# Encoder trunk on one core: dilated V, partial sums and K swaps in fewer transfers, and new priorities and a margin in the order planner

## The chip, the cores and the metric

The kernel runs on one core of a Trainium2 chip. The metric is the device time of one execution in microseconds (us). Engines are named as in the profile: PE is TensorE (PEld its weight loads), DVE is VectorE, ACT is ScalarE, POOL is GpSimd, SP is SyncE, which here issues every DMA (SPq in the rows). All DMAs of the core share 16 DMA engines.

## The reference, cut to what matters

Two request groups, a prompt of 512 rows and a sample of 1024 rows, go through the same two layers with a model width of 1024.

- Layer 0: `h = rms_norm(x)`, `z = h @ w_in0`, split into A (8 query heads over 2 key/value heads, norm on q and k, two-dimensional rotary), B (4 heads of differential attention, two softmaxes subtracted) and a gate; `x + ((A || B) * silu(gate)) @ w_out0`.
- Layer 1: `z = h @ w_in1` gives q, k, v and gate for 16 heads. Attention C has three patterns, (window, dilation) = (128, 1), (512, 4), (2048, 16), each a band in a strided copy of the sequence, merged by their softmax denominators: `o = sum(softmax(lse)[i] * o_i)`. Then `x + (o * silu(gate)) @ w_out1`.

All inputs are fp32. The kernel keeps precision by splitting every fp32 operand into two fp16 parts (high and low) and making three passes of each product (`mm3`, `av`).

## The kernel before, in words

**Units and pieces.** Layer 0 has four A units and four B units, layer 1 has eight C units (two heads each). A unit is made of three pieces of 512 rows (`GRAN`): piece 0 is the prompt, pieces 1 and 2 are the two halves of the sample. `kv_piece` projects K and V of a piece, `qg_piece` q and the gate; `qk_stages` squares, makes 1/rms on POOL (`f_chain`), applies the rotary, splits into fp16 parts and transposes by DMA into `K` or `q` (line 594). The projections of the next unit are merged with the attention steps of this one, so that PE has dense work (line 492) between the short products of the attention.

**Attention step.** Scores on PE into `S` (2 buffers), maximum on DVE, exponential on ACT into `f`, high part on ACT and low part on DVE or POOL into `h` (3 buffers), then a DMA transpose `t<-h` (line 359, called from `t_av`) into `t` (3 buffers, token `t4`), then the product with V on PE (line 784, `av`). `out_tile` has the same transpose for the output projection.

**What C adds.** For the dilated patterns V is needed by class (row modulo 4). Line 682 copies each 128-row tile of `V` into 32 partitions of `Vc`: four transfers for a piece, 96 in all. The dilated partial output lies by class too; `send` (line 1152) puts it back in row order, `pk` to `pn`, in four transfers of 32 partitions, 96 in all. For the scores the two heads' halves of K are also needed swapped: lines 599 and 600 copy partitions 64 to 127 of each new K piece to 0 to 63 of the other slot and the reverse, 78 in all.

**What sets the order.** Nothing is scheduled on the chip. At build time `Plan.run` plays the stages through a model of the engines, with estimated durations and latencies, and writes the instructions in the order in which the model starts them. Each engine, SP too, then runs its own list in that order and only waits for semaphores. Among the stages that are ready, each engine of the model takes the one with the lowest `pos`; `P.pos` grows by 1 with each merged step. A stage that acquires a token starts only when a buffer of that kind is free in the model (`CAPS`). `P.dma` makes three stages: SP issue, DMA, and a latency stage that occupies nothing ("LAT"); the DMA stage can start 0.75 us after the issue (`LAT0`), and the latency is 1.25 us unless a line says otherwise; `P.tdma` is the same for a transpose, with lengths by columns.

**The end of a layer** is written out by hand in `END`: the last units' attention with what projections remain, the weights of the output projection (`wprep`, line 423 its sum of squares, lines 432 to 435 the sum over partitions on PE) and the output tiles.

Of the kernel before, what the change touches and what calls it, by code (L numbers as in the profile page):

```python
# [183 lines left out]


ISSUE = 0.6
PA, PQ, PB = 0, 8, 0
KEEP1 = 1

# [24 lines left out]
def trunk_kernel(ctx: ExitStack, tc: tile.TileContext, A: dict, outs: list):  # L214
    nc = tc.nc
# [298 lines left out]
        return r  # L514


    def qk_stages(zb, ztok, evs, e2, tabs, tdep, ti, kind, isq, dst, dst_acq, dst_use, swap, dst_dep=()):

        b = {}
        t1t, stt_ = Token("t1"), Token("st")  # L520

        def f_sq():
            b["t1"] = new(t1t)
            S_.activation(out=b["t1"], in_=zb["z"], func=AF.Square)
        s = add("ACT", act(512), f_sq, evs, [t1t], [ztok])

        def f_red():
            b["s"] = small(24, "qs", 6)
            V.tensor_reduce(out=b["s"][:, 0:8], in_=b["t1"].rearrange("p h t d -> p (h t) d"), op=AD, axis=AX.X)  # L529
        s = add("DVE", dve(512), f_red, [s], (), [t1t])  # L530

        def f_chain():

            x = b["s"]
            G.tensor_scalar(out=x[:, 8:16], in0=x[:, 0:8], scalar1=1.0 / (64.0 * 4096.0 ** 2), scalar2=e2(), op0=M, op1=AD)  # L535
            rsqrt(x[:, 0:8], x[:, 16:24], x[:, 8:16], 8)
        sr = add("POOL", 3.6, f_chain, [s])

        def t1f():
            return b["t1"].rearrange("p h t d -> p (h t) d")  # L540

        if kind == "A":
            s1t = Token("s1")

            def f_rope():
                gc_t, gs_t = tabs()
                z, t1 = zb["z"], b["t1"]
                s1 = lpool[0].tile([128, 2, 4, 64], F32, tag=f"s1{s1t.slot}", name="s1", bufs=1)
                tt(t1, z, gc_t[:, ti:ti + 4, :].unsqueeze(1).to_broadcast([128, 2, 4, 64]), M)
                zs = z.rearrange("p h t (s y d) -> p (h t s) y d", s=2, y=2)[:, :, ::-1, :]  # L550
                s1v = s1.rearrange("p h t (s y d) -> p (h t s) y d", s=2, y=2)
                for h in range(2):
                    gsv = gs_t[:, ti:ti + 4, :].rearrange("p t (s y d) -> p (t s) y d", s=2, y=2)
                    tt(s1v[:, 8 * h:8 * h + 8], zs[:, 8 * h:8 * h + 8], gsv, M)
                tt(t1, t1, s1, AD)
            sp = add("DVE", 2 * dve(512) + 2 * dve(256) + 0.1, f_rope, [s, tdep], [s1t], [t1t, ztok])

            def f_r():
                tt(t1f(), t1f(), b["s"][:, 0:8].unsqueeze(2).to_broadcast([128, 8, 64]), M)
            s = add("DVE", dve(512), f_r, [sp, sr], (), [t1t])  # L560
        else:
            s1t = Token("s1")

            def f_rope():
                gc_t, gs_t = tabs()[0:2]
                z, t1 = zb["z"], b["t1"]
                tt(t1f(), z.rearrange("p h t d -> p (h t) d"),
                   b["s"][:, 0:8].unsqueeze(2).to_broadcast([128, 8, 64]), M)
                s1 = lpool[0].tile([128, 2, 4, 16], F32, tag=f"s1{s1t.slot}", name="s1", bufs=1)
                ts_ = t1.rearrange("p h t d -> p (h t) d")[:, :, 0:16].rearrange("p a (y d) -> p a y d", y=2)[:, :, ::-1, :]  # L570
                s1v = s1.rearrange("p h t (y d) -> p (h t) y d", y=2)
                for h in range(2):
                    tt(s1v[:, 4 * h:4 * h + 4], ts_[:, 4 * h:4 * h + 4],
                       gs_t[:, ti:ti + 4, :].rearrange("p t (y d) -> p t y d", y=2), M)
                tt(t1[:, :, :, 0:16], t1[:, :, :, 0:16],
                   gc_t[:, ti:ti + 4, :].unsqueeze(1).to_broadcast([128, 2, 4, 16]), M)
                if isq:
                    tt(t1f()[:, :, 16:64], t1f()[:, :, 16:64],
                       tabs()[2][:, 16:64].unsqueeze(1).to_broadcast([128, 8, 48]), M)
                tt(t1[:, :, :, 0:16], t1[:, :, :, 0:16], s1, AD)  # L580
            s = add("DVE", dve(512) + 2 * dve(64) + 2 * dve(128) + 0.3 + (dve(384) if isq else 0.0), f_rope, [sr, tdep], [s1t],
                    [t1t, ztok])

        def f_hi():
            b["st"] = new(stt_)
            S_.activation(out=b["st"][:, :, :, 0:64], in_=b["t1"], func=AF.Copy)
        s = add("ACT", act(512), f_hi, [s], [stt_], [t1t])

        def f_lo():
            tt(b["st"][:, :, :, 64:128], b["t1"], b["st"][:, :, :, 0:64], SU)  # L590
        s = add("DVE", dve(512), f_lo, [s], (), [t1t, stt_])

        def f_T():
            nc.sync.dma_start_transpose(out=dst().rearrange("p h (t q) -> p (h t) q", q=128),
                                        in_=b["st"].rearrange("p h t c -> p (h t c)"))
        s = P.tdma(1024, f_T, [s, dst_dep], dst_acq, tuple(x for x in dst_use if x not in dst_acq) + (stt_,))
        if swap is None:
            return [s]
        w1 = dma(ISSUE, 0.25, lambda: nc.sync.dma_start(out=swap()[0:64], in_=dst()[64:128]), [s], (), dst_use)
        w2 = dma(ISSUE, 0.25, lambda: nc.sync.dma_start(out=swap()[64:128], in_=dst()[0:64]), [s], (), dst_use)  # L600
        return [s, w1, w2]


    class Unit:
        def __init__(self):
# [1 line left out]
            self.qtok, self.sgtok = {}, {}  # L607
            self.k_ready, self.v_ready, self.vc_ready = {}, {}, {}
            self.att_done = {}
            self.Vc = [None, None]  # L610

    last_mm = [None]
    proj_mm = {}
# [10 lines left out]
    def kv_piece(u, gi):  # L624
# [4 lines left out]
        for hf in range(2):  # L629
# [41 lines left out]
                    in1=u.V[:, r:r + 2, 0, :], op0=M, op1=SU)  # L671
            vl = add("DVE", dve(256), f_vl, [vh], (), [pt, u.vtok], pos=P.pos - PB)
            vls.append(vl)
            if u.kind == "C":
                for j in range(2):
                    tl = t0 + 2 * hf + j

                    def f_vc(tl=tl, r=r, j=j):
                        if u.Vc[g] is None:
                            u.Vc[g] = lpool[0].tile([128, g + 1, 4, 256], F16, tag=f"Vc{g + 1}{u.vct[g].slot}", name=f"Vc{g + 1}", bufs=1)  # L680
                        p0 = 32 * (tl % 4)
                        nc.sync.dma_start(out=u.Vc[g][p0:p0 + 32, tl // 4, :, :],
                                          in_=u.V[:, r + j, :, :].rearrange("p a f -> p (a f)"))
                    if tl == 0:
                        u.vc_open = add("NONE", 0.0, None, [vl, u.tdep], [u.vct[g]])
                    vc = dma(ISSUE, 0.25, f_vc, [vl, u.vc_open], (), [u.vct[g], u.vtok])
                    u.vc_ready.setdefault(g, []).append(vc)
        u.v_ready[gi] = vls
        def kdst():
            if not hasattr(u, "K"):  # L690
                u.K = new(u.ktok)
            return u.K[:, 0, gi]
        u.k_ready[gi] = qk_stages(zb, ztok, evs, lambda: u.kvw.e2, lambda: u.ktab, u.tdep, t0, u.kind, False,
                                  kdst, [u.ktok] if gi == 0 else (), [u.ktok], lambda: u.K[:, 1, gi],
                                  () if gi == 0 else u.k_ready[0][0])
        if gi == 2:
            w_done(u.kvw, mms)
# [1 line left out]
    def qg_piece(u, gi):  # L699
# [57 lines left out]
        def qdst():  # L757
            if gi not in u.q:
# [1 line left out]
            return u.q[gi]  # L760
        ti = row // 128 if u.kind == "C" else t0
        u.q_ready[gi] = qk_stages(zb, ztok, evs, lambda: u.qgw.e2, lambda: u.qtab, u.tdep, ti, u.kind, True,
                                  qdst, (), [qt], None)
        if gi == 2:
            w_done(u.qgw, mms)

# [37 lines left out]
    def t_av(u, b, s, h4t, av_fn, av_dur, av_deps, av_acq=(), av_use=()):  # L804
        t4t = Token("t4")

        def f_T():
            b["tt"] = transp(b["hl"], t4t)
        s = P.tdma(2048, f_T, [s], [t4t], [h4t])
        return add("PE", av_dur, av_fn, [s, av_deps], av_acq, [t4t] + list(av_use))  # L810

    def spill(l, u, gi, dep):
# [253 lines left out]
    def att_C(u, gi):  # L1066
# [46 lines left out]
        def p23(hs):  # L1113
            def build():
# [15 lines left out]
                def avf(t4):  # L1130
                    if "o23" not in ob:
                        ob["o23"] = new(ot23).rearrange("p a b -> p (a b)").rearrange("p (c h d) -> p c h d", c=4, h=2)
                    for i, (h, c) in enumerate(blocks):
                        av(ob["o23"][:, c, h, :], t4, i * L // 128, L // 128,
                           lambda k, b: u.Vc[g][:, k, c, 128 * b + 64 * h:128 * b + 64 * h + 64])
                batch(mm, len(blocks) * pe(2 * L, 2), blocks, L, lambda x: u.m23[g][:, t0 // 4, :], mxs,
                      lambda x: ob["md"][:, x[1], 2 + x[0]:3 + x[0]], avf, [u.vc_ready[g]], avs23, ot23)
            return build
# [1 line left out]
        def send():  # L1140
# [2 lines left out]
                S_.activation(out=ob["pk"][:, :, 128:132], in_=ob["md"], func=AF.Copy)  # L1143
                S_.activation(out=ob["pk"][:, :, 0:128], in_=ob["o23"].rearrange("p c h d -> p c (h d)"), func=AF.Copy)
            s = add("ACT", act(512) + 0.12, f_ev, avs23[-1:], [pkt], [ot23])
            s = add("NONE", 0.0, None, [s], [pnt])
            ob["sent"] = []
            for j in range(4):
                def f(j=j):
                    if j == 0:  # L1150
                        ob["pn"] = lpool[0].tile([128, 4, 132], F32, tag=f"pn{pnt.slot}", name="pn", bufs=1)
                    nc.sync.dma_start(out=ob["pn"][:, j, :],
                                      in_=ob["pk"][32 * j:32 * j + 32, :, :].rearrange("p c f -> p (c f)"))
                ob["sent"].append(dma(ISSUE, 0.25, f, [s], (), [pkt, pnt]))
            if gi == 0 or gi == 2:
                close(u.vct[g], avs23)

# [103 lines left out]
    def out_tile(l, g, tl, wo, mix_deps, x_deps, finish):  # L1261
# [31 lines left out]

        def f_T():
            b["tt"] = transp(b["hl"], t4t)
        s = P.tdma(2048, f_T, [s], [t4t], [h4t])

        def f_x():
            x = b["x"] = new(xt)
# [417 lines left out]
```

## Time and profile before

| what | value |
|---|---|
| median of 3 runs | 1854.68 us (1853.79 to 1855.3) |
| profiled execution, its time | 1854.62 us |
| profiled execution, its span | 1852.4 us |
| PE busy | 1675.0 us, 90% |
| DVE / ACT / POOL busy | 1332.2 / 1212.8 / 695.5 us |
| mean granted clock of PE | 0.959 of full speed |

The span runs from the first to the last instruction; the time includes 2.2 us around it. Matmuls are pipelined and their ends are modelled, so the busy time of PE says how much of the span has a matmul in it. An idle time of an engine is put down to what ended it, the releaser.

### The profile page before, as it was taken

The numbers are of one execution on the slowest core, as the hardware profiler recorded it, in microseconds if no ns is written. First come the engines' busy times: TensorE is split into PE (matmuls) and PEld (weight loads), VectorE is DVE, ScalarE is ACT, GpSimd is POOL, SyncE is SP. The second block draws the span as 40 slices with busy tenths as digits, with TensorE's granted clock in tenths as the row PEclk, the third lists the DMA queues.
The fourth block names the chain that finished last, engine by engine and source line by source line (L and its number), as shares of the span: only waits on it lengthen the run. The fifth ranks groups of instructions, "written<-read, shape, count | busy, mean of one in ns | idle before, by whom it ended". The sixth has DMA issues, their size and how long they took to land. (4 is left out here: it accounts for less than half of the span.)

```text
span 1852.4 us, 44798 instructions
## 1 busy us (share of the span) xinstructions
PE 1675.0 (90%) x17626; PEld 1398.4 (75%) x17626; DVE 1332.2 (72%) x2985; ACT 1212.8 (65%) x2593; POOL 695.5 (38%) x1204
## 2 busy tenths in 40 slices
PE   4898978989999999699898999999999999995898
PEld 3776756878887878378787887888788888774788
DVE  7788878767888778965635778677777777787332
ACT  6488978767777767853425676678676757777220
POOL 6523333333463445312212344354444444452200
PEclk9999999999999999799899999999999999996999
DMA  9989999795565445689975676676766757776983
GB/s 251 191 157 166 182 177 167 146 163 113 98 125 101 109 92 122 147 198 224 207 176 128 122 150 131 138 143 140 147 132 144 137 116 151 148 145 140 232 230 103
DMA packets 788724, 282.06 MB, mean 152 GB/s; under 512 B 647072, under 2 KB 772256, under 8 KB 788512
## 3 DMA queue, kind: packets, MB, share of 16 engines
q1 hardware_dynamic: 788512, 279.19, 73.4%
q8 instruction: 138, 2.26, 0.5%
q14 instruction: 74, 0.61, 0.1%
HBM read 73.92 MB, written 25.17 MB: 53 GB/s over the span
## 5 line engine op out<-in xcount | busy, mean ns | idle before, releaser
L492 PE MATMUL pj<-whl,hT 128*128 128x256 f16 x7680 | 882.3, 275 | 22.2 <-DMA hT<-h 21.2
L492 PEld LDWEIGHTS <-hT 128*128 128x128 f16 x7968 | 782.8, 99 | 145.6 <-DMA hT<-h 23.1
L784 PEld LDWEIGHTS <-t 128*128 128x128 f16 x4992 | 200.5, 100 | 93.8 <-DMA t<-h 85.8
L1107 ACT ACTIVATE f<-f,cs,csc 128x256 f32<-128x256 f32 (+1 forms) x384 | 218.4, 570 | 65.5 <-DVE cs L778 65.4
L492 PEld LDWEIGHTS <-t 128*128 128x128 f16 x2304 | 228.9, 100 | 40.0 <-DMA t<-h 9.8
L800 DVE TENSOR_TENSOR h<-f,h 128x1024 f16<-128x1024 f32 x148 | 187.7, 1273 | 57.4 <-ACT h L796 55.0
L784 PE MATMUL pj<-V,t 128*128 128x64 f16 (+1 forms) x4032 | 178.7, 204 | 51.2 <-DMA t<-h 47.8
L492 PE MATMUL pj<-whl,t 128*128 128x256 f16 x1728 | 202.4, 279 | 8.2 <-DMA t<-h 8.2
L772 PE MATMUL S<-K,q 128*128 128x512 f16 x640 | 169.6, 399 | 33.3 <-ACT f L1024 19.1
L796 ACT ACTIVATE h<-f 128x1024 f16<-128x1024 f32 x168 | 175.5, 1051 | 21.9 <-DMA t<-h 19.8
L535 POOL TENSOR_SCALAR qs<-qs,we 128x8 f32<-128x8 f32 x87 | 44.5, 511 | 354.0 <-DVE qs L529 343.1
L261 POOL TENSOR_TENSOR qs<-qs,mhalf 128x8 f32<-128x8 f32 x87 | 147.8, 1699 | 7.3
L772 PEld LDWEIGHTS <-q 128*128 128x128 f16 x640 | 61.0, 101 | 91.7 <-issue 42.8
L854 DVE TENSOR_REDUCE as<-S 128x1 f32<-128x1024 f32 (+1 forms) x80 | 95.9, 1219 | 29.1 <-PE S L772 28.9
L423 ACT ACTIVATE t<-f 128x1024 bf16<-128x1024 f32 x74 | 77.8, 1051 | 44.5 <-DMA f<-in_w_in_dram 32.6
L864 ACT ACTIVATE f<-S,as,asc 128x1024 f32<-128x1024 f32 (+1 forms) x96 | 101.7, 1061 | 4.0 <-DVE h L800 0.5
L478 DVE SCALAR_TENSOR_TENSOR whl<-f,wsm,whl 128x1024 f16<-128x1024 f32 x68 | 87.7, 1305 | 8.2 <-ACT whl L473 8.2
L1332 DVE SCALAR_TENSOR_TENSOR f<-pj,os,f 128x256 f32<-128x256 f32 x96 | 41.9, 479 | 68.0 <-PE pj L492 61.2
L1018 DVE TENSOR_REDUCE bs<-S 128x1 f32<-128x1024 f32 x64 | 77.2, 1217 | 16.2 <-PE S L772 16.2
L800 POOL TENSOR_TENSOR h<-f,h 128x1024 f16<-128x1024 f32 x20 | 43.5, 2175 | 120.9 <-ACT h L796 120.9
L473 ACT ACTIVATE whl<-f,wsm 128x1024 f16<-128x1024 f32 x68 | 75.8, 1140 | 16.8 <-PE pj L492 14.3
L1122 PE MATMUL S<-K,q 128*128 128x256 f16 (+1 forms) x384 | 79.3, 371 | 4.6 <-DVE m L1097 4.6
(250 smaller groups left out, 2684.5 us busy)
## 6 DMA issues: line engine op xcount, KB each, us to landing
f<-in_w_in_dram SPq DMA_DIRECT2D x58, 512.0 KB, 5.3
mixbuf<-sg SPq DMA_DIRECT2D x48, 256.0 KB, 2.8
f<-mixbuf SPq DMA_DIRECT2D x24, 512.0 KB, 5.7
K<-K SPq DMA_DIRECT2D x78, 128.0 KB, 2.5
f<-in_w_out_dram SPq DMA_DIRECT2D x16, 512.0 KB, 4.5
pn<-pk SPq DMA_DIRECT2D x96, 66.0 KB, 2.2
x1buf<-f SPq DMA_DIRECT2D x12, 512.0 KB, 4.1
Vc<-V SPq DMA_DIRECT2D x96, 64.0 KB, 2.3
```

What stands on the lines that cost most here:

```text
L261: G.tensor_tensor(y, v, mhalf[:, 0:n], ALU.pow)
L423: S_.activation(out=junk1(t1t), in_=b[i].rearrange("p k n -> p (k n)"), func=AF.Square, accum_out=b["s"][:, i:i + 1])
L478: stt(out=part(k, 1, i), in0=b[i][:, nk * k:nk * k + nk, :], scalar=sc(), in1=part(k, 0, i), op0=M, op1=SU)
L492: T.matmul(ps, lhs(k, a), wt(k, b), start=(k == 0 and i == 0), stop=(k == 7 and i == 2))
L772: T.matmul(out[:, 512 * i:512 * i + 512], q, u.K[:, st, gi, hk, :], start=(st == 0), stop=(st == 1))
L784: T.matmul(o, t4[:, 8 * a + base + k, :], v(k, b), start=(k == 0 and i == 0), stop=(k == nk - 1 and i == 2))
L796: S_.activation(out=b["hl"][:, 0, :], in_=b["e"], func=AF.Copy)
L800: (G if on_pool else V).tensor_tensor(b["hl"][:, 1, :], b["e"], b["hl"][:, 0, :], SU)
L854: V.tensor_reduce(out=b["s"][:, 0:nh], in_=b["S"].rearrange("p (h k) -> p h k", h=nh), op=ALU.max, axis=AX.X)
L864: S_.activation(out=b["e"][:, w * i:w * i + w], in_=b["S"][:, w * i:w * i + w], func=AF.Exp, bias=b["s"][:, 2 + i:3 + i], scale=u.sc, accu ...
L1107: S_.activation(out=b["e"][:, w * i:w * i + w], in_=b["e"][:, w * i:w * i + w], func=AF.Exp, bias=b["s"][:, i:i + 1], scale=u.sc, accum_ou ...
L1122: T.matmul(s[:, L * i:L * i + L], q, k, start=(sk == 0), stop=(sk == 1))
```

## The change

In the model (`Plan`), which only sets the order:

- the 1/rms chains of `qk_stages` (POOL) get a `pos` lower by 12;
- the transposes of K and q, of the attention tiles (`t_av`) and of the output tiles (`out_tile`) get a `pos` lower by 10;
- behind each transpose of an attention or output tile stands a latency stage of `AHEAD = 2.5` us, in which the `t4` buffer stays taken; the product that reads the tile may start in the model only after it.

In the transfers:

- V by class: one store of the whole piece to a DRAM buffer `vd` (256 KB) and one load back with four rows to a partition, instead of four copies of 64 KB. `Vc` is one tile per piece instead of one per group.
- partial sums: one store of `pk` to a DRAM buffer `pd` and one load into `pn`, instead of four copies; `pn` is now acquired by the load alone.
- K swaps: none after piece 1; after piece 2 both sample pieces are swapped with one pair of transfers of double size.

```diff
+AHEAD = 2.5
@@ qk_stages
-        sr = add("POOL", 3.6, f_chain, [s])
+        sr = add("POOL", 3.6, f_chain, [s], pos=P.pos - 12)
...
-        s = P.tdma(1024, f_T, [s, dst_dep], dst_acq, tuple(x for x in dst_use if x not in dst_acq) + (stt_,))
+        s = P.tdma(1024, f_T, [s, dst_dep], dst_acq, tuple(x for x in dst_use if x not in dst_acq) + (stt_,), pos=P.pos - 10)
         if swap is None:
             return [s]
-        w1 = dma(ISSUE, 0.25, lambda: nc.sync.dma_start(out=swap()[0:64], in_=dst()[64:128]), [s], (), dst_use)
-        w2 = dma(ISSUE, 0.25, lambda: nc.sync.dma_start(out=swap()[64:128], in_=dst()[0:64]), [s], (), dst_use)
-        return [s, w1, w2]
+        return [s] + swap(s)
@@ kv_piece
-            if u.kind == "C":
-                for j in range(2):
-                    tl = t0 + 2 * hf + j
-
-                    def f_vc(tl=tl, r=r, j=j):
...
-                        p0 = 32 * (tl % 4)
-                        nc.sync.dma_start(out=u.Vc[g][p0:p0 + 32, tl // 4, :, :],
-                                          in_=u.V[:, r + j, :, :].rearrange("p a f -> p (a f)"))
-                    if tl == 0:
-                        u.vc_open = add("NONE", 0.0, None, [vl, u.tdep], [u.vct[g]])
-                    vc = dma(ISSUE, 0.25, f_vc, [vl, u.vc_open], (), [u.vct[g], u.vtok])
-                    u.vc_ready.setdefault(g, []).append(vc)
+        if u.kind == "C":
+
+            box["n"] = box.get("n", 0) + 1
+            vd = dr.tile([512, 256], F16, name=f"vd{box['n']}")
+            vs = dma(ISSUE, 0.5, lambda: nc.sync.dma_start(
+                out=vd.rearrange("(t p) f -> p t f", p=128),
+                in_=u.V[:, row // 128:row // 128 + 4].rearrange("p t a f -> p t (a f)")), [vls], (), [u.vtok])
+
+            def f_vc():
+                x = f"Vc{gi}"
+                u.Vc[gi] = lpool[0].tile([128, 4, 256], F16, tag=x, name=x, bufs=1)
+                nc.sync.dma_start(out=u.Vc[gi], in_=vd.rearrange("(p c) f -> p c f", c=4))
+            if t0 == 0:
+                u.vc_open = add("NONE", 0.0, None, [vls, u.tdep], [u.vct[g]])
+            vc = dma(ISSUE, 0.5, f_vc, [vs, u.vc_open], (), [u.vct[g]])
+            u.vc_ready.setdefault(g, []).append(vc)
...
+        def swap(s):
+
+            r = []
+            for a, b in ((0, 64), (64, 0)):
+                def f_w(a=a, b=b):
+                    x = slice(GI[g][0], GI[g][-1] + 1)
+                    nc.sync.dma_start(out=u.K[a:a + 64, 1, x], in_=u.K[b:b + 64, 0, x])
+                r.append(dma(ISSUE, 0.25 + 0.2 * g, f_w, [s, u.k_ready.get(1)], (), [u.ktok]))
+            return r
...
-                                  kdst, [u.ktok] if gi == 0 else (), [u.ktok], lambda: u.K[:, 1, gi],
+                                  kdst, [u.ktok] if gi == 0 else (), [u.ktok], swap if gi != 1 else None,
@@ t_av, and the same two lines in out_tile
-        s = P.tdma(2048, f_T, [s], [t4t], [h4t])
+        s = P.tdma(2048, f_T, [s], [t4t], [h4t], pos=P.pos - 10)
+        s = add("LAT", AHEAD, None, [s], (), [t4t])
@@ att_C, send
-            s = add("NONE", 0.0, None, [s], [pnt])
-            ob["sent"] = []
-            for j in range(4):
-                def f(j=j):
...
-                    nc.sync.dma_start(out=ob["pn"][:, j, :],
-                                      in_=ob["pk"][32 * j:32 * j + 32, :, :].rearrange("p c f -> p (c f)"))
-                ob["sent"].append(dma(ISSUE, 0.25, f, [s], (), [pkt, pnt]))
+            box["n"] = box.get("n", 0) + 1
+            pd = dr.tile([512, 132], F32, name=f"pd{box['n']}")
+            s = dma(ISSUE, 0.5, lambda: nc.sync.dma_start(out=pd.rearrange("(p c) f -> p c f", c=4), in_=ob["pk"]),
+                    [s], (), [pkt])
+
+            def f():
+                ob["pn"] = lpool[0].tile([128, 4, 132], F32, tag=f"pn{pnt.slot}", name="pn", bufs=1)
+                nc.sync.dma_start(out=ob["pn"], in_=pd.rearrange("(j p) f -> p j f", p=128))
+            ob["sent"] = [dma(ISSUE, 0.6, f, [s], [pnt])]
```

## Rows read from the trace of the kernel before

**Rows 1.** The page: span, and busy time of the engines.

```profile
span 1852.4 us, 44798 instructions
PE 1675.0 (90%) x17626; PEld 1398.4 (75%) x17626; DVE 1332.2 (72%) x2985; ACT 1212.8 (65%) x2593; POOL 695.5 (38%) x1204
```

**Rows 2.** Busy time by stretch: stretch and its us, engines, granted clock, DMA share, GB/s.

```profile
100.00:400.00 300.00, 264.08 (x3249) 204.53 (x3247) 244.70 (x319) 247.39 (x434) 102.59 (x117) 0.96 0.91 166
400.00:700.00 300.00, 289.31 (x2815) 238.78 (x2814) 239.63 (x403) 213.02 (x441) 136.72 (x260) 0.98 0.56 109
700.00:800.00 100.00, 79.64 (x654) 57.18 (x652) 87.30 (x141) 81.69 (x163) 43.26 (x80) 0.86 0.63 138
800.00:1000.00 200.00, 181.87 (x1687) 159.14 (x1686) 108.26 (x237) 86.19 (x144) 39.42 (x113) 0.95 0.91 204
1000.00:1600.00 600.00, 575.09 (x6500) 496.15 (x6498) 443.98 (x1346) 414.11 (x1064) 258.88 (x454) 0.99 0.68 135
1600.00:1740.00 140.00, 112.67 (x1244) 94.33 (x1242) 99.02 (x292) 95.62 (x229) 53.85 (x85) 0.87 0.77 158
```

**Rows 3.** Waits of PE, whole span: us in total, times, longest.

```profile
PE pj L784 <- DMA t<-h: 57.1, 53, 4.4
PE S L772 <- ACT f L1024: 19.1, 12, 3.8
PE pj L492 <- DMA t<-h: 8.2, 5, 2.5
```

**Rows 4.** Waits of PE, 100 to 400 us.

```profile
PE pj L784 <- DMA t<-h: 24.7, 22, 2.5
```

**Rows 5.** Waits of PE, 400 to 700 us.

```profile
PE pj L784 <- DMA t<-h: 2.4, 3, 1.3
```

**Rows 6.** Waits of PE, 1000 to 1600 us.

```profile
PE pj L784 <- DMA t<-h: 13.8, 16, 3.2
```

**Rows 7.** SP in order of time near 1100 us: start, us, what.

```profile
1093.83 2.58 SPq L682 DMA_DIRECT2D Vc<-V  x4
1096.52 2.54 SPq L1152 DMA_DIRECT2D pn<-pk  x4
1099.10 2.56 SPq L682 DMA_DIRECT2D Vc<-V  x4
1101.76 1.36 SPq L359 DMA_TRANSPOSE t<-h  x1
```

**Rows 8.** SP in order of time near 1665 us.

```profile
1662.41 5.16 SPq L682 DMA_DIRECT2D Vc<-V  x8
1667.67 0.53 SPq L816 DMA_DIRECT2D mixbuf<-sg  x1
1668.31 2.57 SPq L1152 DMA_DIRECT2D pn<-pk  x4
1670.98 2.64 SPq L359 DMA_TRANSPOSE t<-h  x1
```

**Rows 9.** PE in order of time, the same place; in brackets idle time and releaser.

```profile
1662.22 2.79 PE L492 MATMUL pj<-whl,hT 128*128 128x256 f16 x24
...
1675.64 1.46 PE L784 MATMUL pj<-V,t 128*128 128x64 f16 x24 [4.41 <-DMA t<-h]
```

**Rows 10.** DMA issues: line, count, KB each, median us from issue to landing.

```profile
mixbuf<-sg SPq DMA_DIRECT2D x48, 256.0 KB, 2.8
K<-K SPq DMA_DIRECT2D x78, 128.0 KB, 2.5
pn<-pk SPq DMA_DIRECT2D x96, 66.0 KB, 2.2
Vc<-V SPq DMA_DIRECT2D x96, 64.0 KB, 2.3
```

**Rows 11.** Waits of SP, whole span.

```profile
SPq L599 <- DMA K<-st: 41.6, 19, 3.4
```

**Rows 12.** DMA queue: packets, MB, share of 16 engines over the span.

```profile
q1 hardware_dynamic: 788512, 279.19, 73.4%
```

**Rows 13.** Line 359 alone, 100 to 430 us: issues, then landing min/median/max.

```profile
L359 SPq DMA_TRANSPOSE t<-h x78: 1317/2335/4375, 105.4 to 427.5; - x78
DMA to landing us min/median/max: 4.2/4.9/6.8
```

**Rows 14.** Waits of all engines, whole span.

```profile
POOL cf L1201 <- DMA pn<-pk: 62.1, 12, 25.1
DVE t L567 <- POOL qs L265: 35.1, 31, 3.3
```

More of the change, by code (lines that the diff above doesn't have):

```diff
@@ L514, in h_deps, with qk_stages @@
         return r
-    def qk_stages(zb, ztok, evs, e2, tabs, tdep, ti, kind, isq, dst, dst_acq, dst_use, swap, dst_dep=()):
+    def qk_stages(zb, ztok, evs, e2, tabs, tdep, ti, kind, isq, dst, dst_acq, dst_use, swap=None, dst_dep=()):
         b = {}
@@ L609, in __init__ @@
             self.att_done = {}
-            self.Vc = [None, None]
+            self.Vc = {}
     last_mm = [None]
@@ L673, in kv_piece @@
             vls.append(vl)
-            if u.kind == "C":
-                for j in range(2):
-                    tl = t0 + 2 * hf + j
-                    def f_vc(tl=tl, r=r, j=j):
-                        if u.Vc[g] is None:
-                            u.Vc[g] = lpool[0].tile([128, g + 1, 4, 256], F16, tag=f"Vc{g + 1}{u.vct[g].slot}", name=f"Vc{g + 1}", bufs=1)
-                        p0 = 32 * (tl % 4)
-                        nc.sync.dma_start(out=u.Vc[g][p0:p0 + 32, tl // 4, :, :],
-                                          in_=u.V[:, r + j, :, :].rearrange("p a f -> p (a f)"))
-                    if tl == 0:
-                        u.vc_open = add("NONE", 0.0, None, [vl, u.tdep], [u.vct[g]])
-                    vc = dma(ISSUE, 0.25, f_vc, [vl, u.vc_open], (), [u.vct[g], u.vtok])
-                    u.vc_ready.setdefault(g, []).append(vc)
+        if u.kind == "C":
[12 more added lines that the diff above has]
+            u.vc_ready.setdefault(g, []).append(vc)
         u.v_ready[gi] = vls
@@ L762, in qg_piece @@
         u.q_ready[gi] = qk_stages(zb, ztok, evs, lambda: u.qgw.e2, lambda: u.qtab, u.tdep, ti, u.kind, True,
-                                  qdst, (), [qt], None)
+                                  qdst, (), [qt])
         if gi == 2:
@@ L1134, in avf @@
                         av(ob["o23"][:, c, h, :], t4, i * L // 128, L // 128,
-                           lambda k, b: u.Vc[g][:, k, c, 128 * b + 64 * h:128 * b + 64 * h + 64])
+                           lambda k, b: u.Vc[g + k][:, c, 128 * b + 64 * h:128 * b + 64 * h + 64])
                 batch(mm, len(blocks) * pe(2 * L, 2), blocks, L, lambda x: u.m23[g][:, t0 // 4, :], mxs,
@@ L1145, in send @@
             s = add("ACT", act(512) + 0.12, f_ev, avs23[-1:], [pkt], [ot23])
-            s = add("NONE", 0.0, None, [s], [pnt])
-            ob["sent"] = []
-            for j in range(4):
-                def f(j=j):
-                    if j == 0:
-                        ob["pn"] = lpool[0].tile([128, 4, 132], F32, tag=f"pn{pnt.slot}", name="pn", bufs=1)
-                    nc.sync.dma_start(out=ob["pn"][:, j, :],
-                                      in_=ob["pk"][32 * j:32 * j + 32, :, :].rearrange("p c f -> p (c f)"))
-                ob["sent"].append(dma(ISSUE, 0.25, f, [s], (), [pkt, pnt]))
+            box["n"] = box.get("n", 0) + 1
[6 more added lines that the diff above has]
+            ob["sent"] = [dma(ISSUE, 0.6, f, [s], [pnt])]
             if gi == 0 or gi == 2:
@@ L1295, in f_T @@
             b["tt"] = transp(b["hl"], t4t)
-        s = P.tdma(2048, f_T, [s], [t4t], [h4t])
+        s = P.tdma(2048, f_T, [s], [t4t], [h4t], pos=P.pos - 10)
+        s = add("LAT", AHEAD, None, [s], (), [t4t])
         def f_x():
```

## The prediction, made before the changed kernel was run

> **What bounds the kernel now.** I read the page first. PE has a matmul in 90% of the span, so at most 1852.4 - 1675.0 = 177 us of idle PE can be won back at all, plus whatever its clock loses [rows 1]. DVE at 72% and ACT at 65% follow at a distance. The table of stretches says where that idle time lies [rows 2]. Between 400 and 700 us (B) PE idles 300 - 289.3 = 10.7 us, between 1000 and 1600 us (C) 24.9 us. Between 100 and 400 us (A) it idles 35.9 us while the DMA engines are at 0.91. Around the ends of the layers it idles 20.4, 18.1 and 27.3 us (700 to 800, 800 to 1000, 1600 to 1740), together 65.8 us. The granted clock falls with it: it is 0.98 and 0.99 in the dense stretches and 0.86 and 0.87 at the ends. A stretch at 0.86 has spent part of its time at 1.2 instead of 2.4 GHz; one minus the clock, times the stretch, is the work time lost: 12 us in A, 6 + 6 in the dense ones, 14 + 10 + 18.2 = 42.2 at the ends.
>
> The list of PE's waits then names what ends them [rows 3]. The first by far is the product with V waiting for its transposed tile, 57.1 us in 53 waits, 1.1 us each, 4.4 at most. The same wait of the output tiles is 8.2 us. By stretch the 57.1 us are 24.7 in A [rows 4], 2.4 in B [rows 5], 13.8 in C [rows 6], and so 16.2 at the ends.
>
> The order of SP shows why tiles come late. Near 1100 us twelve small copies in a row take 7.7 us of SP before a transpose gets its turn [rows 7]. Near 1665 us eight of `Vc`, a spill and four of `pn` take from 1662.41 to 1670.88, and the transpose behind them [rows 8] is the one for which PE idles 4.41 us [rows 9]. SP takes its list strictly in order, so a transpose pays for what stands ahead of it, issue time and waits alike.
>
> **The margin and the priorities.** `AHEAD` adds no wait on the chip; it only writes the product later in PE's list, behind work that the model has at hand. In the dense stretches such work is there (a projection group of 24 matmuls is 2.8 us [rows 9]), and a mean wait of 1.1 us is shorter than the 2.5 us. Of the 2.4 + 13.8 us there I count 0.9 as gone: 14.6 us. In A I count half of 24.7, 12.3 us, because the DMA engines at 0.91 leave that stretch only 27 us to shrink, and because the tile buffers are held longer (below). At the ends PE has little else to do, so the wait mostly stays under another name; 0.4 of 16.2 + 8.2 = 24.4 is 9.8 us. Sum 36.7 us; bounds 0 and all 65.3.
>
> With the idle time goes its share of the lost clock, in the proportion of idle time removed: A 12.3/35.9 of 12 = 4.1, dense 14.6/35.6 of 12 = 4.9, ends 9.8/65.8 of 42.2 = 6.3, together 15.3 us. Bounds 0 and, were all the waits gone, 8.3 + 5.5 + 15.6 = 29.4.
>
> The priority of the 1/rms chain on POOL shortens a wait of DVE, 35.1 us in all [rows 14]; DVE is busy for 72% and seldom the one PE waits for, so it counts nothing. If DVE became the bound this would be worth at most those 35 us.
>
> What the later place costs: a product that slips behind a 2.8 us group at an end makes its piece finish later. Two units by three pieces by two layers are 12 pieces, so between 0 and 12 x 2.8 = 33.6 us; I take a quarter, 8, since there PE waits for data more often than data for PE.
>
> **The transfers.** SP issues 78 + 96 + 96 = 270 of the three kinds before [rows 10]. After, K needs 2 for each of 26 pieces instead of 39, that is 52; V two for each of 24 pieces, 48; the partial sums 48. 122 issues fewer, at 0.64 us each (7.7 us for twelve, [rows 7]) 78 us of SP. It has no term of its own: what it brings PE is late transposes no longer late, which the 36.7 us hold already, and it is why I count anything at the ends. The Trainium skill, DMA: Bandwidth & Descriptors, section "Issuing engines are not separate DMA queues", speaks against it: the time to initiate a DMA is usually small relative to the DMA itself. For one copy the rows agree (0.64 us against a landing of 2.2 us, [rows 7, 10]), for a row of twelve ahead of a transpose they do not; by the rule the ends' 9.8 + 6.3 us would fall away and the sum would come to about 1837.
>
> Against it stands a new dependence: a load from DRAM may be issued only when the store has landed, and SP stands still until then, with all transposes behind it. No row shows it; the nearest is the K swap, which waits on SP for its transpose: 41.6 us over 39 pairs, 1.07 us each, 3.4 at most [rows 11]. 48 stores at that price are 51 us of SP, and 13 pairs fewer give 14 back. On balance SP gains 78 + 14 - 51 = 41 us, so I let only 6 of the 51 reach PE (bounds 0 and 51). A store's landing is nearest to `mixbuf<-sg`, also 256 KB into DRAM: 2.8 us [rows 10]; the model reckons 0.75 + 0.5 + 1.25 = 2.5, so it errs by little.
>
> The detour doubles the bytes: 24 x 262 KB + 24 x 270 KB = 12.8 MB more. The queue moves 279.19 MB in 73.4% of 1852 us, 205 GB/s [rows 12], so 62 us more of all 16 engines, 0.08 on top of the 0.68 in layer 1 [rows 2]. A at 0.91 has 24.7/3 = 8.2 us of tile waits per 100 us, C at 0.68 has 13.8/6 = 2.3 [rows 2, 4, 6]; between the two, 0.08 costs 2.1 per 100 us, 17 us over the 814 us in which these transfers lie. The margin hides most of it; I take 4 (bounds 0 and 17).
>
> The partial sums come later: four issues and 2.2 us, 4.8 in all, become 0.64 + 2.8 + 0.64 + about 2.5, 6.6 us. The one who waits is POOL, 62.1 us already [rows 14], at 38% busy and covered by the two near-band batches that follow `send`: nothing. Without that cover it is 24 x 1.8 = 43 us of POOL. The K pair of double size lands some 0.3 us later (256 against 128 KB, [rows 10]); sample scores needed both pieces before, too, and come a unit later: nothing.
>
> **Sum.** 36.7 + 15.3 - 8 - 6 - 4 = 34 us. From the profiled execution's 1854.6 us (the median of the runs is 0.1 above it) that gives **1820.6 us**, say 1821.
>
> **Rivals.**
>
> *The waits only change their name.* DVE and ACT are at 82% in A and 87% and 82% between 700 and 800 us [rows 2]; if they set the pace there, PE is given a projection now and lacks it later. Then only the dense stretches gain, 14.6 + 4.9, against 18 of costs: 1853 us. For it speaks that scores also wait for ACT (19.1 us, [rows 3]); against it, that this is a third of the tile waits.
>
> *SP stands still for the stores (slower).* If the landing is longer than what the model leaves, all 51 us reach PE instead of 6: 1821 + 45 = 1866 us. It decides when a store holds SP for longer than the margin covers, 2.5 us; the longest wait of the nearest row is 3.4, the mean 1.07 [rows 11]. The Trainium skill, same page, section "Two DMAs through the same engine are not ordered", asks for this very wait: the issuing engine has to wait for the first DMA's semaphore before it issues the dependent one. That it is there is sure; its length no run here shows yet.
>
> *The three tile buffers bind in A (slower).* 78 tiles are issued in 322 us there [rows 13], so three buffers allow a hold of 3 x 322/78 = 12.4 us. The hold is about 4.9 (landing) + 1.1 (wait) + 0.9 (product), with the margin 9.4 us. It decides when landings reach 7.9 us; the longest in A is 6.8 [rows 13]. At 9.6 the hold is 14.1, A takes 367 us, 45 more, and its gain of 16.4 is lost: up to 1882 us, about 1860 in the middle.
>
> **How the numbers follow.** What this kernel's measurement can tell from no change is about 0.2%, 3.7 us. The forecast, 1795 to 1842 us, has 0.60. A greater gain, towards all 65.3 us and their clock (1760), has 0.05. Waits that change their name have 0.16, around 1853: 0.05 faster, 0.09 same, 0.02 slower. The stores have 0.08. The tile buffers have 0.11, of which 0.02 end faster, where the hold just touches its limit. So faster 0.60 + 0.05 + 0.05 + 0.02 = 0.72, same 0.09, slower 0.02 + 0.08 + 0.09 = 0.19. The range runs from 1790, below which lies the 0.05, to 1857, above which lie most of the two slower cases, 0.15. The forecast's own range is 1795 to 1842.
>
> **What the profile after would show.** PE's wait for `t<-h` down from 65 us to about 29, in C to under 3; the clock at the ends up to about 0.9; 148 issues of the three kinds; SP waiting for `vd` and `pd` about 1 us a time; a DMA share in C of about 0.76. I am wrong if A gets longer, if SP's waits for the stores pass 50 us, or if PE's waits for scores grow by as much as those for tiles fall.

## The result, and the profile after

The changed kernel takes 1831.3 us (median; 1827.7 to 1832.5) against 1854.5 us, a ratio of 0.9883 with a 95% interval of 0.9861 to 0.9904: 23 us faster where 34 were forecast, inside the range. The profiled execution has a span of 1830.7 us, 21.7 less than [rows 1].

The page after, span and busy time of the engines:

```profile
span 1830.7 us, 44605 instructions
PE 1661.4 (91%) x17626; PEld 1397.2 (76%) x17626; DVE 1332.9 (73%) x2985; ACT 1210.3 (66%) x2593; POOL 718.9 (39%) x1204
```

PE does the same 17626 matmuls, so the span splits in two. Busy time fell from 1675.0 to 1661.4, 13.6 us. Idle time fell from 177.4 to 169.3 us, 8.1 only. Together they are the 21.7 us.

This compares two single executions. That the 13.6 us are matmuls that run at 2.4 instead of 1.2 GHz is not shown. The mean granted clock is 0.964 after and 0.959 before in these two; over the four runs of the changed kernel it is 0.958 to 0.964, mean 0.962, and over the 61 runs of the kernel before that stand beside the experiments 0.956 to 0.970, mean 0.963. `e1_margin_only` below also has only 1662.5 us of busy time, at a clock of 0.956, and is not faster.

Busy time by stretch, columns as in [rows 2] (what falls into a stretch shifts a little, since the kernel is shorter):

```profile
100.00:400.00 300.00, 261.65 (x3209) 203.72 (x3207) 249.12 (x320) 243.97 (x429) 111.82 (x118) 0.96 0.93 166
400.00:700.00 300.00, 287.75 (x2798) 236.41 (x2796) 237.37 (x393) 209.43 (x432) 144.86 (x252) 0.98 0.57 108
700.00:800.00 100.00, 80.10 (x686) 59.33 (x684) 87.38 (x140) 79.96 (x160) 42.09 (x77) 0.88 0.66 135
800.00:1000.00 200.00, 186.18 (x1733) 162.78 (x1731) 116.31 (x250) 95.17 (x162) 45.34 (x124) 0.97 0.91 211
1000.00:1600.00 600.00, 577.92 (x6607) 503.55 (x6606) 443.17 (x1367) 422.26 (x1087) 267.31 (x464) 0.98 0.75 154
1600.00:1740.00 140.00, 116.34 (x1296) 99.97 (x1294) 97.07 (x292) 92.06 (x217) 49.71 (x81) 0.89 0.89 201
```

A did not gain: 3209 matmuls in those 300 us, 3249 before. C gained a little, 6607 against 6500 in the same 600 us, with the DMA engines at 0.75 instead of 0.68. In these two executions the clock is higher by 0.02 in each of the three stretches at the ends, and not in A or C.

The waits of PE after, whole span (line 795 is the old 784, 783 the old 772, 493 the old 492, 1036 and 876 the old 1024 and 864):

```profile
PE S L783 <- ACT f L1036: 27.9, 16, 6.1
PE S L783 <- ACT f L876: 26.0, 21, 3.4
...
PE pj L795 <- DMA t<-h: 18.0, 16, 5.1
...
PE pj L493 <- DMA t<-h: 2.8, 2, 2.4
```

The waits for tiles fell from 57.1 + 8.2 to 18.0 + 2.8 us [rows 3], 44.5 less. But the scores' waits for ACT rose, and between 100 and 400 us they took the tiles' place. Before, then after:

```profile
PE S L772 <- ACT f L864: 10.6, 8, 2.3
```

```profile
PE S L783 <- ACT f L876: 26.0, 21, 3.4
PE pj L795 <- DMA t<-h: 5.8, 7, 1.5
```

The tiles' 24.7 us there [rows 4] became 5.8, and the scores' wait for the exponential, which reads one of the two `S` buffers, went from 10.6 to 26.0. The tiles no longer come late; the scores do.

In the same stretch SP waits longer for the products, which are what frees a tile buffer for the next transpose. Before, then after:

```profile
SPq L359 <- PE pj L784: 29.9, 16, 3.7
```

```profile
SPq L360 <- PE pj L795: 47.9, 23, 5.3
```

SP's waits after, whole span, the two for the stores:

```profile
SPq L1165 <- DMA pd<-pk: 28.2, 15, 4.0
SPq L684 <- DMA vd<-V: 26.9, 12, 4.1
```

DMA issues after: line, count, KB each, us to landing.

```profile
K<-K SPq DMA_DIRECT2D x26, 256.0 KB, 4.0
...
Vc<-vd SPq DMA_DIRECT2D x24, 256.0 KB, 2.8
```

The stores hold SP for 28.2 + 26.9 = 55.1 us, about the 51 that the prediction priced.

### The profile page after: what moved, and what is told of

The parts are those of the page before. It is cut to its first block, busy times and chain, and to the rows that moved or that the text cites. A ratio compares the mean times of both kernels' runs of the same rounds, so it can differ in the third digit from the quotient of the medians.

```text
span 1830.7 us, 44605 instructions
## 1 busy us (share of the span) xinstructions
PE 1661.4 (91%) x17626; PEld 1397.2 (76%) x17626; DVE 1332.9 (73%) x2985; ACT 1210.3 (66%) x2593; POOL 718.9 (39%) x1204
## 4 chain that ended last, share of the span: by engine, by line
PE 36%; DMA 6%; DVE 4%; POOL 2%; ACT 2%; issue 1%; SPq 1%; DVEq 0%; POOLq 0%; ACTq 0%
PE pj L493 28%; PE S L1134 3%; PE pj L795 2%; DMA t<-h 2%; PE pj L507 2%; DVE f L1109 1%; PE S L1182 1%; DMA x1buf<-f 1%; ACT f L1119 1%; DMA pn<-pd 1%; DMA cqg<-in_c_q_norm_dram 0%; DVE h L811 0%; POOL sg L1249 0%; DMA f<-in_w_out_dram 0%; POOL pn L1248 0%
## 5 line engine op out<-in xcount | busy, mean ns | idle before, releaser
L493 PE MATMUL pj<-whl,t 128*128 128x256 f16 x1728 | 197.0, 275 | 6.2 <-DVE os L1294 3.4
L536 POOL TENSOR_SCALAR qs<-qs,we 128x8 f32<-128x8 f32 x87 | 50.2, 577 | 363.6 <-DVE qs L530 346.8
L783 PEld LDWEIGHTS <-q 128*128 128x128 f16 x640 | 61.9, 101 | 122.9 <-issue 76.2
L424 ACT ACTIVATE t<-f 128x1024 bf16<-128x1024 f32 x74 | 78.0, 1054 | 63.0 <-DMA f<-in_w_in_dram 47.9
L866 DVE TENSOR_REDUCE as<-S 128x1 f32<-128x1024 f32 (+1 forms) x80 | 96.4, 1219 | 27.2 <-PE S L783 26.9
L1109 DVE CUSTOM_DVE_ANT_0 f<-S,mask 128x256 f32<-128x256 f32 x192 | 69.7, 420 | 20.3 <-PE S L1182 20.0
```

The lines of the kernel that those rows point to most:

```text
L493: T.matmul(ps, lhs(k, a), wt(k, b), start=(k == 0 and i == 0), stop=(k == 7 and i == 2))
L783: T.matmul(out[:, 512 * i:512 * i + 512], q, u.K[:, st, gi, hk, :], start=(st == 0), stop=(st == 1))
L866: V.tensor_reduce(out=b["s"][:, 0:nh], in_=b["S"].rearrange("p (h k) -> p h k", h=nh), op=ALU.max, axis=AX.X)
L1109: V.tensor_tensor_reduce(out=b["e"][:, w * i:w * i + w], in0=b["S"][:, w * i:w * i + w], in1=mask(x), scale=1.0, scalar=-3.0e38, op0=AD, o ...
```

## The experiments

The question was which part brings the gain. The theory, from the prediction, was the margin; the rivals were the freed SP queue and the priorities. All ratios are to the kernel before, run beside it on the same chip, with 95% intervals.

**The parts by themselves.**

`e1_margin_only`, the kernel before with

```diff
+AHEAD = 2.5
-        s = P.tdma(2048, f_T, [s], [t4t], [h4t])
+        s = P.tdma(2048, f_T, [s], [t4t], [h4t])
+        s = add("LAT", AHEAD, None, [s], (), [t4t])
```

> The kernel before with the 2.5 us margin behind attention and output tiles, nothing else of the change. Theory (the margin brings the gain): about 1835 us, PE's waits for tiles down from 65 to about 22 us, and between 100 and 400 us down from 24.7 to about 6 with the waits for scores up from 10.6 to about 26, so that this stretch ends no earlier. Rival (the freed SP queue brings it): within 5 us of 1854. Rival (the priorities bring it): the same 1854.

Measured: 1.0037 (1.0016 to 1.0058). The margin alone does not make the kernel 20 us faster; it is a little slower. The theory falls, though between 100 and 400 us the profile does what was foreseen: the tiles' wait is 3.5 us and the scores' 27.3. Over the whole span the waits for tiles are 24.2 + 6.2 us, more than the 22 expected. PE's waits of this run between 1000 and 1600 us (line 785 is the product, 750 the gate on DVE):

```profile
PE pj L785 <- DVE sg L750: 23.7, 5, 6.4
...
PE pj L785 <- DMA t<-h: 1.9, 3, 0.7
```

The waits for tiles go from 13.8 [rows 6] to 1.9 us, and in their place stands a new one of 23.7 us. The product line here waits for a DVE instruction that reads a `pj` buffer, of which there are four: probably a later product finds no `pj` free. The mean granted clock is lower, too: 0.954 over the ten runs, 0.962 over the 19 of the kernel before beside them.

`e2_prio_only`, the kernel before with `pos=P.pos - 12` on the 1/rms chain and `pos=P.pos - 10` on the transposes.

> The kernel before with the two priorities only. Theory (margin): within 6 us of 1854, waits for tiles still 55 to 65 us. Rival (priorities): 1835 to 1840 us, tiles' waits halved because transposes are issued sooner.

Measured: 1.0035 (1.0013 to 1.0057), and the waits for tiles are 76.2 + 7.2 us, more than before. The priorities bring nothing by themselves.

`e3_transfers_only`, the changed kernel without the margin and both priorities.

> The kernel before with the new transfers only (V and partial sums by way of DRAM, fewer K swaps). Theory (margin): about 1850 us, the waits for tiles in layer 1 down by a few us, SP waiting some 50 us for the stores. Rival (the freed SP queue brings the gain): about 1835 us, nearly all of it in the last third. Rival (the stores hold SP up): 1860 us or more.

Measured: 1837.8 us, 0.9911 (0.9881 to 0.9940). The rival has it: most of the gain is in the transfers.

`e4_after_no_margin`, the changed kernel without the two lines `s = add("LAT", AHEAD, ...)`.

> The changed kernel without the margin, priorities and transfers kept. Theory (margin): 1848 to 1854 us, waits for tiles back at 50 us or more. Rival (transfers or priorities bring the gain): 1828 to 1836 us, as the changed kernel.

Measured: 1833.8 us, 0.9882 (0.9853 to 0.9912), the changed kernel's ratio. Its waits for tiles are four times those of the changed kernel, in the same total time:

```profile
PE pj L795 <- DMA t<-h: 81.2, 55, 11.2
...
PE pj L493 <- DMA t<-h: 10.7, 3, 5.7
```

Beside this run the margin has 128 matmuls more done in the first 1000 us (8941 against 8813) and 81 fewer in the next 600 (6607 against 6688): it shifts the work and gains nothing in all. So the wait for tiles, the first of PE's list, is not what sets this kernel's time.

**Which transfer.** The theory now: SP's issue time. Of 122 issues taken away V has 48, the partial sums 48, K 26.

`e5_v_only`, `e6_pn_only`, `e7_k_only`: the kernel before with the hunk on `Vc`, on `pn` or on the swaps alone, as in the diff above.

> The kernel before with V by class by way of DRAM, nothing else. Theory (SP's issue time counts): the gain of the three transfers, some 17 us, is shared by issues taken away, 48 of 122: about 7 us, 1848. Rival (the partial sums' path counts): within 3 us of 1855. Rival (only the order was shuffled): anywhere within 8 us of 1855, and the three parts don't add up to 17.

> The kernel before with the partial sums by way of DRAM, nothing else. Theory (SP's issue time counts): 48 of 122 issues, about 7 us, 1848. Rival (the partial sums' path counts: pk is free as soon as its store has landed and pn is taken by the load alone): 1838 to 1843 us, most of it in the last 200 us. Rival (order shuffled): anywhere within 8 us of 1855.

> The kernel before with the K swaps after pieces 0 and 2 only. Theory (SP's issue time counts): 26 of 122 issues and 13 waits, about 4 us, 1851. Rival (the partial sums' path): 1855. Rival (order shuffled): anywhere within 8 us of 1855.

Measured: V 0.9874 (0.9859 to 0.9890), the partial sums 1.0018 (0.9994 to 1.0042), K 1.0048 (1.0023 to 1.0073). V alone takes 1823.7 us, 25 less than the 1849.2 us beside it (23 by the ratio), no less than the three together. The partial sums take as many issues away and bring nothing. A price per issue doesn't explain that.

`e8_split_loads`: the three transfers without margin and priorities, the loads back of V and of the partial sums cut in four, with the model told so.

```diff
-                nc.sync.dma_start(out=u.Vc[gi], in_=vd.rearrange("(p c) f -> p c f", c=4))
+                for i in range(4):
+                    nc.sync.dma_start(out=u.Vc[gi][32 * i:32 * i + 32],
+                                      in_=vd[128 * i:128 * i + 128, :].rearrange("(p c) f -> p c f", c=4))
-            vc = dma(ISSUE, 0.5, f_vc, [vs, u.vc_open], (), [u.vct[g]])
+            vc = dma(4 * ISSUE, 0.5, f_vc, [vs, u.vc_open], (), [u.vct[g]])
...
-                nc.sync.dma_start(out=ob["pn"], in_=pd.rearrange("(j p) f -> p j f", p=128))
+                for j in range(4):
+                    nc.sync.dma_start(out=ob["pn"][:, j, :], in_=pd[128 * j:128 * j + 128, :])
-            ob["sent"] = [dma(ISSUE, 0.6, f, [s], [pnt])]
+            ob["sent"] = [dma(4 * ISSUE, 0.6, f, [s], [pnt])]
```

> All three transfers as in the changed kernel, without margin and priorities, but each load back from DRAM in four issues instead of one (the same bytes): 144 issues more, 22 more than in the kernel before. Theory (SP's issue time counts): the gain is gone, 1852 to 1862 us, with PE's waits for tiles in layer 1 up again. Rival (the partial sums' path, or fewer waits, count): stays within 5 us of 1838.

Measured: 1.0124 (1.0097 to 1.0151). The gain is gone and more. `e9_v_split` does the same to V alone:

> V by class by way of DRAM alone, as in the run that did only that, but the load back in four issues of 32 partitions instead of one: 120 issues on this way against 48, and against 96 copies before; same bytes, same detour. Theory (SP's issue time counts): the gain goes, 1850 to 1862 us. Rival (V's way by DRAM itself helps, for instance by freeing V or by fewer transfers in flight): stays at 1822 to 1830 us. Rival (a lucky order): anything between.

Measured: 1.0029 (1.0011 to 1.0046). Cutting one load in four, on the chip and in the model, costs the whole 25 us of V, so the detour by DRAM is not the gain.

**The issue time, or the order?** Each edit so far also changed the order that the model writes. `e10_shuffled_before` and `e11_shuffled_v` change only that, in the kernel before and in V alone:

```diff
-ISSUE = 0.6
+ISSUE = 0.66
```

> The kernel before, with one number of the order model changed and nothing else: an issue on SP is reckoned as 0.66 instead of 0.60 us. Instructions and transfers are the same, only their order differs. Theory (SP's issue time counts): the time stays within 6 us of the kernel before, which shows how much a shuffled order alone is worth. Rival (a lucky order explains the differences of 5 to 25 us): it moves by 10 us or more.

> V by class by way of DRAM alone, with the same shuffle of the order as in the other run, an issue reckoned as 0.66 us. Theory (SP's issue time counts): 1822 to 1832 us, the gain stays. Rival (a lucky order gave V its 25 us): back to 1840 us or more.

Measured: 0.9929 (0.9903 to 0.9955) for the kernel before, 0.9833 (0.9809 to 0.9857) for V. The first goes to the rival: the same instructions in another order are worth 0.7%, 13 us. The second goes to the theory: V keeps most of its gain, 0.0096 (about 0.0035 either way) below its partner, where it was 0.0126. The single numbers of the margin, the priorities, the partial sums and K, all under 0.5%, are within that.

`e12_v_same_order` then holds the order fixed. It is V alone with

```diff
-            vc = dma(ISSUE, 0.5, f_vc, [vs, u.vc_open], (), [u.vct[g]])
+            vc = dma(4 * ISSUE, 0.5, f_vc, [vs, u.vc_open], (), [u.vct[g]])
```

so that every engine's list is that of `e9_v_split`, except that 24 loads stand where 96 stood. The two traces bear this out: apart from these loads, the five engines' lists agree entry by entry.

> V by class alone, one load back as in the run of V alone, but the model reckons that load as four issues. So every engine's list is the same, entry for entry, as in the run with the split load, and the chip issues 72 DMAs fewer. Theory (the chip's SP time counts): 1822 to 1835 us, as V alone. Rival (what counts is the order that the model writes when it believes SP to be free): 1848 to 1862 us, as the split load.

Measured: 0.9979 (0.9959 to 0.9998). The rival has most of it. From `e9_v_split` the 72 issues fewer, with the same bytes in larger loads, give 0.0050 (about 0.0026 either way), 9 us. From here to V alone, where the chip executes the same instructions and only the model believes SP to be free sooner, so that the order differs, it is another 0.0105 (about 0.0025), 19 us.

The stretch from 1000 to 1600 us shows it, columns as in [rows 2]. `e9_v_split`, then `e12_v_same_order`, then `e5_v_only`, then `e10_shuffled_before`, then `e11_shuffled_v`:

```profile
1000.00:1600.00 600.00, 575.76 (x6479) 495.28 (x6476) 441.92 (x1332) 410.11 (x1055) 260.19 (x452) 0.98 0.71 142
```

```profile
1000.00:1600.00 600.00, 577.23 (x6500) 498.22 (x6495) 442.16 (x1337) 411.21 (x1058) 258.71 (x454) 0.98 0.70 142
```

```profile
1000.00:1600.00 600.00, 590.58 (x6775) 514.45 (x6773) 459.06 (x1408) 432.02 (x1112) 259.78 (x472) 1.00 0.75 149
```

```profile
1000.00:1600.00 600.00, 582.08 (x6674) 505.54 (x6671) 449.79 (x1357) 419.92 (x1081) 273.50 (x468) 0.99 0.69 138
```

```profile
1000.00:1600.00 600.00, 590.60 (x6772) 513.59 (x6771) 456.62 (x1397) 430.03 (x1107) 259.37 (x476) 1.00 0.75 149
```

V alone, shuffled or not, has PE idle for 9.4 us there at a granted clock of 1.00, and gets 6775 and 6772 matmuls done. With the load reckoned as four issues PE idles 22.8 us at 0.98 and does 6500, as before the change (24.9 us, 0.99 and 6500, [rows 2]).

Over all runs: the kernels whose model reckons V's way back as one issue (the changed one, e3, e4, e5, e11) lie at 0.9833 to 0.9911. Those with four (e1, e2, e6 to e10, e12, and the kernel before at 1) lie at 0.9929 to 1.0124. The two groups' ratios don't overlap, though the intervals of `e3_transfers_only` and `e10_shuffled_before` do. This speaks against mere luck of the order, but since one harmless shuffle moves 13 us, how much of the 19 us would stay with other orders is not shown.

The lists in the traces say where the orders differ. From V alone to `e12_v_same_order` the tile transposes of layer 1 move on average by less than one place in SP's list, while in PE's list the scores of layer 1 stand on average 17 matmuls earlier and the products 4 earlier. Of the twelve kernels without the margin, e3, e4, e5 and e11 have these scores at a mean place of 12880 to 12881 in PE's list, e10 at 12874, the seven slower ones at 12835 to 12865. But the changed kernel, with the margin, has them at 12831 and is as fast as V alone, so the place of the scores goes with the time without being shown as the cause.

## Why the prediction was right, point by point, and where its reasons were not

**The outcome** was right in sign and range. The sum was 34 us, measured 23; the cause was largely another, so that the number fell inside the range is in good part luck. Of the sum 36.7 + 15.3 - 8 = 44 us hang on the margin, which brought nothing that could be measured; the transfers, for which it took off 6 + 4 = 10 us, brought the gain.

**The margin, 36.7 us of idle time.** This is the step that failed. "PE's wait for `t<-h` down from 65 us to about 29" came out at 20.8, C "under 3" at 4.8. But idle time fell by 8.1 us in all, the margin alone gave 0.4% more time, and taking it out of the changed kernel changed nothing; the 13 us that a shuffled order can move are too few to hide 44 us in both. That work is at hand in PE's list when a tile is late was right; that PE is not short of it afterwards was wrong. A wait named by its releaser is not a gain: what the work is taken for is missing later, as a score that finds no `S` buffer emptied by the exponential (A: 10.6 to 26.0 us) or a `pj` buffer that isn't free (e1: 23.7 us).

**The clock, 15.3 us.** Not shown, and with the margin the clock went the other way. The two profiled executions differ by 13.6 us of busy time, in size as forecast, but over its runs the changed kernel has no higher clock than the kernel before (0.962 and 0.963). Where the margin was added the mean clock fell: from 0.962 to 0.954 in `e1_margin_only`, and from 0.970 in the four runs of `e4_after_no_margin` to 0.962 in the changed kernel's four, which did not run side by side. A has 0.96 both times and C went from 0.99 to 0.98, where 9 of the 15.3 us were put. Nor is one minus the clock, times the stretch, work time lost, as the term had it: `e1_margin_only` has a lower clock than the kernel before (0.956 and 0.959, profiled) and 12.5 us less of busy time.

**The rival of the waits that change their name,** given 0.16 and 1853 us, was the truer account of the margin: in A it is what the profile shows. Its sign, that the waits for scores grow by as much as those for tiles fall, nearly came there (15.4 up, 18.9 down) but not in the whole span (24.2 up for the two scores' waits on ACT, 44.5 down). It lacked the gain from the transfers.

**The priorities** counted nothing. By themselves they measured 1.0035, inside what a shuffle moves.

**The transfers: "no term of its own".** Wrong for V, which measured 25 us alone; right for the partial sums (0.9994 to 1.0042). The reason given, issue time ahead of a transpose [rows 7, 8], is real and worth some 9 us for 72 issues. The Trainium skill, DMA: Bandwidth & Descriptors, section "Issuing engines are not separate DMA queues", calls the time to initiate a DMA usually small relative to the DMA itself. For one load of V the rows agree: 338 ns of issue, 2.8 us to landing. The larger part, 19 us between two kernels with the same instructions, is the order that follows from what the model reckons for SP. What in those lists helps PE stays open.

**SP standing still for the stores:** 55.1 us measured, 51 priced. By the prediction's own sign (past 50 us) it was to be wrong; yet the kernel is faster, so these waits don't all reach PE. **The DMA share:** 0.75 in C, 0.76 forecast. **The three tile buffers in A** bound more than before, since SP's waits for products rose from 29.9 to 47.9 us (22.8 in `e4_after_no_margin`), but did not set A's length, as that rival had it: POOL's last tile of A starts at 425.0 us against 424.2, where up to 45 us more was feared. **The K pair** lands in 4.0 us, not 0.3 later than 2.5; K alone measured 1.0048, and whether that is the landing or a shuffle stays open.

## What to carry to other kernels

When a list scheduler (a program that plans the order at build time, as `Plan.run` does here) fixes the order, first run the old kernel with one harmless number of its model changed: here that moved the time by 0.7%, and no smaller effect of a single edit can be read as the edit's own. A transfer's cost is then twofold, what the chip spends on it and what the model reserves for it; hold the order and change the instructions, or the reverse, to tell them apart. And the largest wait of the bottleneck engine is only a gain if something else isn't due at the same moment: cut to a quarter by the margin, from `e4_after_no_margin` to the changed kernel, it left the time where it was.

V by class alone does as well as the whole change: 0.9874 against 0.9883. With an issue reckoned as 0.66 us it has 0.9833 (1824.9 us), the lowest of all, by no more than a shuffle can move.

## What was unexpected of the hardware

The issue time on SP does not follow the bytes. By the median, the 64 KB copies into 32 partitions took 603 ns each, the 256 KB load of four rows to a partition 338 ns, its quarters of 64 KB 417 ns, and the 256 KB store of 512-byte rows 525 ns. What it does follow is open: the 264 KB load of 528-byte rows took 371 ns. The issues of the 256 KB load in the changed kernel: shortest, median and longest in ns, first and last start:

```profile
L684 SPq DMA_DIRECT2D Vc<-vd x24: 332/338/570, 933.1 to 1654.6; - x24
```
